# First feed-forward block: up projections as seven half-block products, residual stream in DRAM, down projections between the products

## Chip, cores and metric

The kernel runs on one core of a Trainium2 chip. The metric is device time in microseconds (us), from the program's start to its end. The core has TensorE (PE, matrix products into PSUM), VectorE (DVE), ScalarE (ACT), GpSimd (POOL), and SyncE (SP), whose queue issues the transfers (DMA) between DRAM and the on-chip memory SBUF.

## What is computed

One layer of a diffusion backbone over 512 latent and 256 context tokens of width 1024: a feed-forward half step, a mixing block (gated linear attention and differential attention), a second feed-forward half step and a final norm. The change concerns the first half step alone, which both kinds of token pass with the same weights and with modulations of their own:

```python
def _swiglu(h, w1, w3, w2):
    return (jax.nn.silu(h @ w1) * (h @ w3)) @ w2
...
xl = xl + 0.5 * ml[2] * _swiglu(_modnorm(xl, ffn1_norm[i], ml[0], ml[1]), ffn1_w1[i], ffn1_w3[i], ffn1_w2[i])
xc = xc + 0.5 * mc[2] * _swiglu(_modnorm(xc, ffn1_norm[i], mc[0], mc[1]), ffn1_w1[i], ffn1_w3[i], ffn1_w2[i])
```

`w1` and `w3` are 1024 x 2816, `w2` is 2816 x 1024, all in float32; `ml` and `mc` are the nine adaLN modulations.

## The kernel before

Activations lie with the model dimension on the 128 partitions: `xl` (8 k-tiles x 512 latent tokens) and `xc` (8 x 256 context tokens) stay in SBUF through the block. A float32 product is made of three passes in the float32r format: each operand is split into a high part (ACT copies it) and a low part (DVE subtracts), and PE adds low x high, high x low and high x high. `wload` fetches 512 KB of weights on SP into one of two `raw` buffers, and ACT (L117) and DVE (L118) split them into `whi` and `wlo`, three buffers of each.

The hidden width of 2816 is 22 blocks (f) of 128. For each f, `Ffn.up` runs two weights x 8 k x 3 passes, each a pair of matmuls of 512 and 256 columns (`mm_k`, L246 and L249), into the PSUM tiles `h13`; `act` then forms silu on ACT (L282), the product on DVE (L285) and its parts `gh` and `gl` (L286, L287), which are kept in a ring of eight. The f-blocks are gathered in `CHUNKS` of 6, 6, 5 and 5. Once a chunk is complete, `down` goes over the 8 output tiles m: 5 or 6 f accumulate in a PSUM tile `dn` of two buffers (L123 to L125), and DVE adds it, times the gate, into `xl` and `xc` (L303). The last chunk comes after all up projections, first for the latent tokens, whose norm follows, and then for the context tokens.

Beside this, `more_ada` makes the modulations that are needed later: 56 rows of the adaLN weights come through four buffers `adaw`, and DVE forms 80 dot products from them (`ada_dot`, L133). Ahead of it all the first tokens are normalised and modulated (`mod_h`) k by k, while PE already runs f = 0 on the tiles that are ready. The order of the instructions on each engine is set by a scheduler, which moves weight loads and their splits ahead of other work (`high_priority`); each engine then runs in that order. Tiles with one or two buffers are handed on when their last reader is done.

## Time and profile before

| | us |
|---|---|
| times of three runs | 1791.6, 2190.8 (median), 5782.49 |
| profiled execution, its own time | 1785.35 |
| its span, first to last instruction | 1783.6 |
| PE, DVE, ACT, POOL busy in it | 1738.2, 1000.3, 629.1, 111.6 |

The profile is of one execution, and the durations in this text are from it. The three times differ widely, and the profiled execution's is near the lowest. An engine's busy time is an average over the whole span; what bounds a stage is read from the windows and the waits of that stage. The first feed-forward block takes about the first 605 us: the tokens' norm up to 30, the up projections from there to 555, and the last chunk to 605.

### The profile page before, as it was taken

How to read it: one execution, taken by the hardware profiler on the slowest of the kernel's cores; microseconds unless marked ns; L12 is line 12 of the kernel's file. 1: busy time of each engine (PE TensorE's matmuls, PEld its weight loads, DVE VectorE, ACT ScalarE, POOL GpSimd, SP SyncE). 2: the span in 40 equal slices, each digit the busy share in tenths (PEclk: the TensorE clock that was granted, in tenths of full speed). 3: DMA queues.
4: the chain of work that ended last, by engine and by line, in shares of the span. 5: the costliest groups of instructions: out<-in, count | busy, mean ns of one | idle time of the engine just before them, and what ended most of it. 6: DMA issues, size and time to landing. Idle time of an engine off the chain costs nothing.

```text
span 1783.6 us, 24883 instructions
## 1 busy us (share of the span) xinstructions
PE 1738.2 (97%) x10184; PEld 1523.1 (85%) x10184; DVE 1000.3 (56%) x1666; ACT 629.1 (35%) x940; POOL 111.6 (6%) x190
## 2 busy tenths in 40 slices
PE   6999999999999999999999899999999999999998
PEld 4788888888888889899888789998888988888887
DVE  5554454354445757877755776767655733333445
ACT  3311122111112435555664543434423332222233
POOL 3100000000000400000000212121001100000000
PEclk9999999999999999999999899999999999999999
DMA  8333344244242444423322112122554233333231
GB/s 331 133 117 108 108 139 152 71 135 155 77 154 63 156 133 113 115 82 93 113 83 82 36 60 71 30 67 83 168 159 135 72 92 98 96 94 107 83 115 63
DMA packets 61986, 193.62 MB, mean 109 GB/s; under 512 B 8488, under 2 KB 8744, under 8 KB 60592
## 3 DMA queue, kind: packets, MB, share of 16 engines
q1 hardware_dynamic: 61872, 192.03, 34.2%
q8 instruction: 80, 1.31, 0.3%
q14 instruction: 34, 0.28, 0.0%
HBM read 168.93 MB, written 8.39 MB: 99 GB/s over the span
## 4 chain that ended last, share of the span: by engine, by line
PE 89%; DVE 3%; ACT 1%; issue 1%; POOL 1%; DMA 1%; DVEq 0%; ACTq 0%; POOLq 0%
PE h L249 22%; PE h L246 11%; PE pl L249 8%; PE dn L123 5%; PE dn L124 5%; PE dn L125 5%; PE pl L246 4%; PE pb L249 3%; PE ptm L505 3%; PE ptm L504 3%; PE ptm L506 3%; PE S L613 3%; PE po L249 2%; PE pb L246 1%; PE pa L956 1%; PE pc L249 1%
## 5 line engine op out<-in xcount | busy, mean ns | idle before, releaser
L117 ACT ACTIVATE whi<-raw 128x1024 fp32r<-128x1024 f32 (+2 forms) x246 | 241.1, 983 | 509.1 <-PE dn L125 191.6
L118 DVE TENSOR_TENSOR wlo<-raw,whi 128x1024 fp32r<-128x1024 f32 (+2 forms) x231 | 262.1, 1137 | 219.7 <-ACT whi L117 218.2
L246 PE MATMUL h<-hH,wlo 128*128 128x512 f32 (+1 forms) x704 | 273.3, 388 | 1.9 <-ACT hH L221 1.4
L249 PE MATMUL h<-hL,whi 128*128 128x512 f32 (+1 forms) x704 | 274.5, 390 | 0.6 <-DVE hL L222 0.6
L249 PE MATMUL h<-hH,whi 128*128 128x512 f32 (+1 forms) x704 | 273.2, 388 | 0.0
L249 PE MATMUL h<-hC,whi 128*128 128x256 f32 x704 | 196.9, 280 | 0.0
L123 PE MATMUL dn<-gh,wlo 128*128 128x512 f32 (+1 forms) x568 | 194.5, 343 | 0.6 <-ACT gh L286 0.4
L124 PE MATMUL dn<-gl,whi 128*128 128x512 f32 (+1 forms) x568 | 194.1, 342 | 0.0
L125 PE MATMUL dn<-gh,whi 128*128 128x512 f32 (+1 forms) x568 | 193.6, 341 | 0.0
L246 PEld LDWEIGHTS h<-hH,wlo 128*128 128x128 f32 x704 | 132.2, 188 | 33.1 <-ACT hH L221 2.4
L249 PEld LDWEIGHTS h<-hH,whi 128*128 128x128 f32 x704 | 132.3, 188 | 29.6
L249 PEld LDWEIGHTS h<-hL,whi 128*128 128x128 f32 x704 | 132.3, 188 | 28.2 <-DVE hL L222 1.0
L246 PE MATMUL pl<-hH,wlo 128*128 128x512 f32 x328 | 131.8, 402 | 8.2 <-DVE sg L838 5.1
L285 DVE TENSOR_TENSOR g<-s,h 128x512 f32<-128x512 f32 (+2 forms) x46 | 36.2, 791 | 182.2 <-PE h L249 110.0
L249 PEld LDWEIGHTS h<-hC,whi 128*128 128x128 f32 x704 | 133.0, 189 | 0.7 <-DVE hC L222 0.4
L249 PE MATMUL pl<-hL,whi 128*128 128x512 f32 x328 | 130.6, 398 | 0.0
L249 PE MATMUL pl<-hH,whi 128*128 128x512 f32 x328 | 130.2, 397 | 0.0
L123 PEld LDWEIGHTS dn<-gh,wlo 128*128 128x128 f32 x568 | 107.6, 190 | 13.6 <-ACT gh L286 0.6
L125 PEld LDWEIGHTS dn<-gh,whi 128*128 128x128 f32 x568 | 107.5, 189 | 12.4
L124 PEld LDWEIGHTS dn<-gl,whi 128*128 128x128 f32 x568 | 107.6, 190 | 12.2
L505 PE MATMUL ptm<-wlo,hH 128*128 128x256 f32 x384 | 110.4, 288 | 5.3 <-DVE wlo L118 5.3
L504 PE MATMUL ptm<-whi,hL 128*128 128x256 f32 x384 | 111.7, 291 | 0.0
(267 smaller groups left out, 3315.6 us busy)
## 6 DMA issues: line engine op xcount, KB each, us to landing
raw<-win SPq DMA_DIRECT2D x65, 512.0 KB, 3.6
adaw<-ada SPq DMA_DIRECT2D x56, 512.0 KB, 4.4
raw<-f1w SPq DMA_DIRECT2D x44, 512.0 KB, 3.6
raw<-f2w SPq DMA_DIRECT2D x44, 512.0 KB, 3.5
aw<-ada SPq DMA_DIRECT2D x8, 1024.0 KB, 9.9
raw<-wbr SPq DMA_DIRECT2D x16, 512.0 KB, 3.7
raw<-f1w SPq DMA_DIRECT2D x16, 384.0 KB, 3.4
raw<-wout SPq DMA_DIRECT2D x12, 512.0 KB, 3.5
```

The costliest lines, as they stand in the source:

```text
L117: S.activation(hi[:, :w], raw[:, :w], AF.Copy)
L118: ld = (eng or V).tensor_tensor(lo[:, :w], raw[:, :w], hi[:, :w].bitcast(F32), op=ALU.subtract)
L123: PE.matmul(out_, wl, xh, start=first, stop=False)
L124: PE.matmul(out_, wh, xlo, start=False, stop=False)
L125: PE.matmul(out_, wh, xh, start=False, stop=last)
L246: PE.matmul(dst(o0, n), wl[:, ks], h.at(0, k, o0, n), start=(k == 0), stop=False)
L249: mm = PE.matmul(dst(o0, n), wh[:, ks], h.at(i, k, o0, n), start=False, stop=(k == KT - 1 and i == 0))
L285: self.mark = V.tensor_tensor(g[:, sl], s[:, sl], pts[1][:, sl], op=ALU.mult).ins
L504: PE.matmul(o_, tl, wh[:, cs], start=f, stop=False)
L505: PE.matmul(o_, th, wl[:, cs], start=False, stop=False)
L506: PE.matmul(o_, th, wh[:, cs], start=False, stop=l)
L613: PE.matmul(sp[:, n0:n1], QQ[:, q, c, qs], KK[:, c, n0:n1], start=q == 1, stop=q == 0)
```

## The change

The change makes blocks f = 0 and 1 as before, on two token halves of 384 (256 latent and 128 context tokens each). The other 20 blocks go in ten pairs p. For a pair and one of the two weights (a *unit*; i = 0 is `w1`, i = 1 is `w3`) the operands are cut in 2 x 2: the model dimension in halves of 4 k-tiles, the outputs in two f, the tokens in two halves. The four output quarters come from seven products instead of eight (Strassen's scheme in Winograd's form); a product (`prod`) is 4 k x 3 passes = 12 matmuls of 384 columns. That takes sums and differences of the tokens (`Tq`, formed and split once) and of the weights (`prep`, four DVE additions of 512 columns for each unit, of tiles `X`, `Y`, `L` and `A`, whose splits go to the ring of `whi` and `wlo`, or in `late` to spare room in the tiles that hold the tokens). ACT copies three intermediate states of the accumulation out of PSUM (`c1`, `c2`, `c3`), and DVE adds what is missing to each output.

`xl` and `xc` no longer stay in SBUF. `xs` in DRAM starts as a copy of the input. A down projection now covers a pair (2 f): PE runs it in pieces between the products (0, 4 and 8 pieces in the first three units, 4 in each of the next fifteen, none in the last two), ACT takes each piece times the gate out of PSUM into `yd` (two buffers), and POOL issues a transfer of 384 KB that adds it to `xs` in DRAM. For the last chunk, of four f, `xl` and `xc` are read back from `xs`. `adaw` has two buffers instead of four, the dots' results go to the one-buffer tile `Y` that `prep` uses, and `mod_h` for the first tokens becomes `tok`, with four parts of 384 columns.

The core of the diff:

```diff
+CHUNKS1 = [(f, 2) for f in range(0, 18, 2)] + [(18, 4)]
+TH, LH, CH = T // 2, TL // 2, TC // 2
...
-        w = pool_.tile([P, D], F32, tag="adaw", name=u("adaw"), bufs=4)
+        w = pool_.tile([P, D], F32, tag="adaw", name=u("adaw"), bufs=2)
...
-            jk = pool_.tile([P, D], F32, tag="adaj", name=u("adaj"), bufs=2)
+            jk = junk()
...
+        def tok(k):
+
+            for i, (x_, R_) in enumerate(((xlat[:, k], R[0]), (xctx[:, k], R[1][:, :TC]))):
+                V.scalar_tensor_tensor(x_, x_, modA[:, i, k:k + 1], halves(R_), op0=ALU.mult, op1=ALU.mult)
+                S.activation(x_, x_, AF.Identity, bias=mods[:, k, i:i + 1])
+            for t in range(2):
+                hh, hl = (h1.at(i, k, t * TH, TH) for i in range(2))
+                S.activation(hh, xT[:, k, t], AF.Copy)
+                V.tensor_tensor(hl, xT[:, k, t], hh.bitcast(F32), op=ALU.subtract)
...
+    def sums():
+        return sf.tile([P, D], F32, tag="Y", name=u("Y"), bufs=1)
...
+    def split_q(i):
+        S.activation(Tq[i][0], q_[i], AF.Copy)
+        V.tensor_tensor(Tq[i][1], q_[i], Tq[i][0].bitcast(F32), op=ALU.subtract)
...
+    def prep(p, i):
+        X = wp.tile([P, 1024], F32, tag="raw", name=u("raw"), bufs=RB)
+        L = sf.tile([P, 1024], F32, tag="L", name=u("L"), bufs=1)
+        A = sf.tile([P, 512], F32, tag="A", name=u("A"), bufs=1)
+        Y = sums()
+        l, r = slice(0, 512), slice(512, 1024)
+        with tc.high_priority(offset=WPRI):
+            SY.dma_start(X[:, l], w13[2 * p, i][:, l])
+            SY.dma_start(A, w13[2 * p + 1, i][:, l])
+            SY.dma_start(L[:, r], w13[2 * p + 1, i][:, r])
+            SY.dma_start(L[:, l], w13[2 * p, i][:, r])
+            V.tensor_tensor(X[:, r], A, L[:, r], op=ALU.add)
+            V.tensor_tensor(Y[:, l], X[:, l], X[:, r], op=ALU.add)
+            V.tensor_tensor(Y[:, r], X[:, l], A, op=ALU.add)
+            V.tensor_tensor(A, Y[:, l], L[:, l], op=ALU.add)
+            return ring_w(X), ring_w(Y), L, A
+
+    def late(w):
+        with tc.high_priority(offset=WPRI):
+            return split_w(w[2], spare[1], spare[2]), split_w(w[3], spare[0][:, :512], spare[0][:, 512:])
...
+    def unit(p, i, w, fills, nxt):
...
+        L, S4 = late(w)
+        prod(pa, X, 0, B[0], True)
+        c1 = small("c1")
+        S.activation(c1, pa, AF.Copy)
+        prod(pf, X, 512, Tq[0], True)
+        prod(pa, Y, 0, Tq[3], False)
+        c2 = small("c2")
+        S.activation(c2, pa, AF.Copy)
+        for f in fills[:len(fills) // 2]:
+            f()
+        if not fills:
+            prod(pe, L, 0, B[2], True)
+            out(0, c1, False, pe)
+        prod(pa, Y, 512, Tq[1], False)
+        c3 = small("c3")
+        S.activation(c3, pa, AF.Copy)
+        for f in fills[len(fills) // 2:]:
+            f()
+        nw = prep(*nxt) if nxt else None
+        out(3, c3, True, pf)
+        more_ada()
+        prod(pa, L, 512, Tq[2], False)
+        out(2, None, True, psum=pa)
+        if fills:
+            prod(pe, L, 0, B[2], True)
+            out(0, c1, False, pe)
+        prod(pf, S4, 0, B[3], False)
+        out(1, c2, False, pf)
+        return nw
...
+    def down_add(p, m, wd):
+
+        if m % 4 == 0:
+            wd[0] = wload(w2d[:, 2 * p * D + m * 256:2 * p * D + (m + 4) * 256])
+        y = sr.tile([P, 2, TH], F32, tag="yd", name=u("yd"), bufs=2)
+        for i, seg in enumerate((LAT, CTX)):
+            S.activation(y[:, :, seg[0]], down(2 * p, 2, wd[0], m % 4 * 256, seg), AF.Copy, scale=gate[:, i, m:m + 1])
+        G.dma_start(xs[:, m], y, accum_op=ALU.add)
...
+    with tc.high_priority(offset=WPRI):
+        for m in range(KT):
+            SY.dma_start(halves(xl[:, m, :]), xs[:, m, :, :LH])
+        for m in range(KT):
+            SY.dma_start(halves(xc[:, m, :]), xs[:, m, :, LH:])
```

ACT in the middle of the block, before: the queue holds a silu (`s`), a high part (`gh`) and four weight splits (`whi`) for each f.

```order
L117 ACTIVATE whi418_3000<-raw417_2999 128x1024
L282 ACTIVATE s404_2975<-h13396_2865 128x768
L117 ACTIVATE whi421_3054<-raw420_3053 128x1024
L117 ACTIVATE whi437_3132<-raw436_3131 128x1024
L286 ACTIVATE gh406_2977<-g405_2976 128x768
L282 ACTIVATE s423_3107<-h13415_2997 128x768
L117 ACTIVATE whi440_3186<-raw439_3185 128x1024
L117 ACTIVATE whi456_3264<-raw455_3263 128x1024
L286 ACTIVATE gh425_3109<-g424_3108 128x768
```

ACT in the middle of the block, after; `whi546` and `whi548` are the splits of X and Y, `yd` the evacuations of down pieces:

```order
L491 ACTIVATE whi546_3321<-raw542_3309 128x1024
L570 ACTIVATE c2525_3215<-st522_3171 128x384
L617 ACTIVATE yd529_3223<-dn530_3224,gate_80 128x2x256
L617 ACTIVATE yd529_3223<-dn531_3232,gate_80 128x2x128
L617 ACTIVATE yd532_3241<-dn533_3242,gate_80 128x2x256
L617 ACTIVATE yd532_3241<-dn534_3250,gate_80 128x2x128
L578 ACTIVATE c3535_3271<-st522_3171 128x384
L491 ACTIVATE whi548_3325<-Y545_3312 128x1024
L617 ACTIVATE yd536_3273<-dn537_3274,gate_80 128x2x256
L555 ACTIVATE gh486_2954<-s483_2951 128x384
L617 ACTIVATE yd536_3273<-dn538_3282,gate_80 128x2x128
L617 ACTIVATE yd539_3291<-dn540_3292,gate_80 128x2x256
```

The copies c2 and c3, which PE's next product waits for, now stand behind a weight split, and the evacuations behind the copies, with c3 between the second and the third piece.

DVE in the middle of the block, before: weight splits (`wlo`), the products `g` and `gl`, and dots (`adaj`).

```order
L118 TENSOR_TENSOR wlo265_1841<-raw263_1839,whi264_1840 128x1024
L118 TENSOR_TENSOR wlo268_1895<-raw266_1893,whi267_1894 128x1024
L285 TENSOR_TENSOR g251_1816<-s250_1815,h13243_1706 128x768
L133 SCALAR_TENSOR_TENSOR adaj255_1825,mods_78<-adaw254_1823,sc_89 128x1024
L287 TENSOR_TENSOR gl253_1818<-g251_1816,gh252_1817 128x768
L133 SCALAR_TENSOR_TENSOR adaj256_1827,mods_78<-adaw254_1823,sc_89 128x1024
L133 SCALAR_TENSOR_TENSOR adaj258_1831,mods_78<-adaw257_1829,sc_89 128x1024
L133 SCALAR_TENSOR_TENSOR adaj260_1835,mods_78<-adaw259_1833,sc_89 128x1024
```

DVE at the end of a w3 unit, after; `hC3` and `hH1` receive the late splits of L and A, `raw506` and `Y509` are the sums X and Y for the next unit:

```order
L548 TENSOR_TENSOR c1449_2746<-c1449_2746,pe448_2729 128x384
L492 TENSOR_TENSOR hC3_90<-L468_2867,hL2_89 128x1024
L553 TENSOR_TENSOR s410_2512<-s410_2512,c1449_2746 128x384
L492 TENSOR_TENSOR hH1_88<-A469_2868,hH1_88 128x512
L548 TENSOR_TENSOR c2450_2772<-c2450_2772,st447_2728 128x384
L556 TENSOR_TENSOR gl412_2514<-s410_2512,gh411_2513 128x384
L553 TENSOR_TENSOR s410_2512<-s410_2512,c2450_2772 128x384
L114 TENSOR_TENSOR wlo492_3002<-raw490_3000,whi491_3001 128x1024
L556 TENSOR_TENSOR gl412_2514<-s410_2512,gh411_2513 128x384
L134 TENSOR_TENSOR mods_78<-mods_78,vec_76 128x16 x2
L509 TENSOR_TENSOR raw506_3092<-A508_3094,L507_3093 128x512
L511 TENSOR_TENSOR Y509_3095<-raw506_3092,A508_3094 128x512
```

The late split of A, the outputs c1, c2 and `gl`, the down weights' split and the next unit's first sum now stand in one queue, in this order.

SP at the end of the block, before: the last chunk's weights, then those of the mixing block.

```order
L116 DMA raw_4534<-f1w 128x640
L116 DMA raw_4560<-f1w 128x640
L116 DMA raw_4743<-f1w 128x640
L116 DMA raw_4773<-f1w 128x640
L116 DMA raw_4803<-f1w 128x640
L116 DMA raw_4859<-win 128x1024
L457 DMA xsp<-xl 128x4096
```

SP there, after:

```order
L507 DMA L_4817<-f1w 128x512
L506 DMA A_4818<-f1w 128x512
L508 DMA L_4817<-f1w 128x512
L112 DMA raw_5038<-f1w 128x512
L112 DMA raw_5061<-f1w 128x512
L112 DMA raw_5084<-f1w 128x512
L112 DMA raw_5107<-f1w 128x512
L657 DMA xl<-xs 128x2x256 x8
L659 DMA xc<-xs 128x2x128 x8
L112 DMA raw_5130<-f1w 128x512
L112 DMA raw_5153<-f1w 128x512
```

The 16 reads of `xl` and `xc` stand between the last chunk's weights, ahead of those of its fifth tile and all later ones.

## Rows read from the trace of the kernel before

**Rows 1.** The page, part 1: busy us (share of the span) and instructions of each engine.
```profile
PE 1738.2 (97%) x10184; PEld 1523.1 (85%) x10184; DVE 1000.3 (56%) x1666; ACT 629.1 (35%) x940; POOL 111.6 (6%) x190
```

**Rows 2.** The page, part 4: the chain that ended last, by line.
```profile
PE h L249 22%; PE h L246 11%; PE pl L249 8%; PE dn L123 5%; PE dn L124 5%; PE dn L125 5%; PE pl L246 4%; PE pb L249 3%; PE ptm L505 3%; PE ptm L504 3%; PE ptm L506 3%; PE S L613 3%; PE po L249 2%; PE pb L246 1%; PE pa L956 1%; PE pc L249 1%
```

**Rows 3.** Windows: us, busy time of each engine, granted clock, DMA share, GB/s.
```profile
30.50:58.00 27.50, 25.52 (x190) 18.03 (x187) 18.10 (x36) 13.02 (x23) 8.40 (x20) 1.00 0.52 198
100.00:164.00 64.00, 64.00 (x368) 55.89 (x367) 31.05 (x46) 13.81 (x16) 0.00 (x0) 1.00 0.42 130
30.50:602.00 571.50, 567.62 (x3288) 491.58 (x3285) 284.30 (x423) 130.03 (x168) 22.72 (x30) 1.00 0.38 123
```

**Rows 4.** Waits, 30 to 600 us: total, times, longest.
```profile
ACT s L282 <- PE h L249: 136.2, 22, 7.4
...
PE h L246 <- ACT hH L221: 1.4, 2, 0.8
```

**Rows 5.** Timeline of ACT, 100 to 140 us: start, duration, instruction.
```profile
100.98 0.81 ACT L282 ACTIVATE s<-h 128x768 f32<-128x768 f32 x1 [6.48 <-PE h L249]
...
117.62 0.81 ACT L282 ACTIVATE s<-h 128x768 f32<-128x768 f32 x1 [6.47 <-PE h L249]
```

**Rows 6.** Timeline of PE, 168 to 172 us, a down projection.
```profile
168.02 0.39 PE L123 MATMUL dn<-gh,wlo 128*128 128x512 f32 x1
168.25 0.39 PE L124 MATMUL dn<-gl,whi 128*128 128x512 f32 x1
...
169.50 0.28 PE L124 MATMUL dn<-gl,whi 128*128 128x256 f32 x1
169.62 0.28 PE L125 MATMUL dn<-gh,whi 128*128 128x256 f32 x1
```

**Rows 7.** Groups by line and shape, 0 to 605 us: busy, mean ns, idle before.
```profile
L133 DVE SCALAR_TENSOR_TENSOR adaj<-adaw,sc 128x1024 f32<-128x1024 f32 x80 | 94.4, 1221 | 0.0
...
L118 DVE TENSOR_TENSOR wlo<-raw,whi 128x1024 fp32r<-128x1024 f32 x40 | 50.3, 1258 | 56.3 <-ACT whi L117 56.3
...
L117 ACT ACTIVATE whi<-raw 128x1024 fp32r<-128x1024 f32 x46 | 48.3, 1055 | 131.7 <-PE h L249 80.6 <-PE dn L125 44.4 <-issue 6.6
...
L287 DVE TENSOR_TENSOR gl<-g,gh 128x768 fp32r<-128x768 f32 x21 | 20.1, 955 | 0.2 <-ACT gh L286 0.2
...
L287 DVE TENSOR_TENSOR gl<-g,gh 128x512 fp32r<-128x512 f32 x1 | 0.7, 683 | 0.0
...
L282 ACT ACTIVATE s<-h 128x512 f32<-128x512 f32 x1 | 0.6, 598 | 0.7 <-PE h L249 0.7
...
L287 DVE TENSOR_TENSOR gl<-g,gh 128x256 fp32r<-128x256 f32 x1 | 0.4, 419 | 0.0
...
L282 ACT ACTIVATE s<-h 128x256 f32<-128x256 f32 x1 | 0.4, 380 | 0.0
```

**Rows 8.** DMA issues: KB each, median us from issue to landing.
```profile
adaw<-ada SPq DMA_DIRECT2D x56, 512.0 KB, 4.4
raw<-f1w SPq DMA_DIRECT2D x44, 512.0 KB, 3.6
...
raw<-f1w SPq DMA_DIRECT2D x16, 384.0 KB, 3.4
...
mgd<-mg SPq DMA_DIRECT2D x16, 256.0 KB, 2.0
...
xsp<-xl SPq DMA_DIRECT2D x1, 2048.0 KB, 9.2
...
mgl<-mgd SPq DMA_DIRECT2D x8, 256.0 KB, 3.5
```

**Rows 9.** Timelines of DVE and POOL, 595 to 601 us.
```profile
595.74 0.75 DVE L222 SCALAR_TENSOR_TENSOR hL<-h,mods,hH 128x512 fp32r<-128x512 f32 x1
...
599.26 2.21 DVE L222 SCALAR_TENSOR_TENSOR hL<-h,mods,hH 128x512 fp32r<-128x512 f32 x1
...
598.51 2.41 POOL L118 TENSOR_TENSOR wlo<-raw,whi 128x1024 fp32r<-128x1024 f32 x1 [0.23 <-ACT whi L117]
```

More of the change, by code (lines that the diff above doesn't have):

```diff
@@ L410, in layer, with more_ada @@
-    ffn_es = ExitStack()
-    f1.fp = ffn_es.enter_context(tc.tile_pool(name="ffn1", bufs=1))
-    f1.act(0, pts)
-    lat_part = lambda m: (xl[:, m, :], 0, TL, gate[:, 0, m:m + 1])
-    ctx_part = lambda m: (xc[:, m, :], TL, TC, gate[:, 1, m:m + 1])
-    f1.run(1, lambda m: [lat_part(m), ctx_part(m)], more_ada)
+    def more_ada():
+        if pairs:
+            for j in pairs[:2]:
+                ada_dot(adp, sums, sc, j, (0, 1))
+                if j < 24:
+                    G.tensor_scalar(mods[:, j, :], mods[:, j, :], vec[:, V_BADA + j:V_BADA + j + 1], None,
+                                    op0=ALU.add)
+                    G.tensor_scalar(gate[:, 0:2, j - 16], mods[:, j, :], 0.5, None, op0=ALU.mult)
+            del pairs[:2]
+        else:
+            for j in ones_[:4]:
+                ada_dot(adp, sums, sc, j, (0,))
+            del ones_[:4]
@@ new lines, in late, with prod @@
+    def late(w):
+        with tc.high_priority(offset=WPRI):
+            return split_w(w[2], spare[1], spare[2]), split_w(w[3], spare[0][:, :512], spare[0][:, 512:])
+    def prod(dst, w, c0, op, first):
+        for k in range(4):
+            ks = slice(c0 + k * P, c0 + (k + 1) * P)
+            hi, lo = w[0][:, ks], w[1][:, ks]
+            bh, bl = op[0][:, k, :], op[1][:, k, :]
+            PE.matmul(dst, lo, bh, start=first and k == 0, stop=False, skip_group_check=True)
+            PE.matmul(dst, hi, bl, start=False, stop=False, skip_group_check=True)
+            mm = PE.matmul(dst, hi, bh, start=False, stop=k == 3, skip_group_check=True)
+        return mm.ins
@@ new lines, in layer, with small, out @@
+    ss = {}
+    def small(tag):
+        return sr.tile([P, TH], F32, tag=tag, name=u(tag), bufs=1)
+    def unit(p, i, w, fills, nxt):
+        t = big(u("st"))
+        pa, pf, pe = t[:, :TH], t[:, 512:512 + TH], sm(u("pe"))[:, :TH]
+        X, Y = w[0], w[1]
+        def out(q, c, neg, add=None, psum=None):
+            f, h = 2 * p + q // 2, q % 2
+            sq = s[:, q, :]
+            if i == 0:
+                if psum is None:
+                    V.tensor_tensor(sq, c, add, op=ALU.add)
+                return S.activation(sq, sq if psum is None else psum, AF.Silu, scale=-1.0 if neg else 1.0)
+            if psum is None:
+                V.tensor_tensor(c, c, add, op=ALU.add)
+            src = c if psum is None else psum
+            if neg:
+                V.scalar_tensor_tensor(sq, src, -1.0, sq, op0=ALU.mult, op1=ALU.mult)
+            else:
+                V.tensor_tensor(sq, sq, src, op=ALU.mult)
+            gh, gl = (g[:, h, :] for g in ring[f])
+            S.activation(gh, sq, AF.Copy)
+            V.tensor_tensor(gl, sq, gh.bitcast(F32), op=ALU.subtract)
+        if i == 0:
+            s = ss[p] = thp.tile([P, 4, TH], F32, tag="s", name=u("s"), bufs=2)
+            new_g(2 * p)
+            new_g(2 * p + 1)
+        s = ss[p]
+        L, S4 = late(w)
[27 more added lines that the diff above has]
+        return nw
@@ new lines, in layer, with down_w, down @@
+    w2d = a["f1w2"]
+    def down_w(f0, nf, m, eng=None, hold=None):
+        off = f0 * D + m * nf * P
+        return wload(w2d[:, off:off + nf * P], nf * P, eng, hold)
+    LAT, CTX = (slice(0, LH), TL), (slice(LH, TH), TC)
+    def down(f0, nf, w, c0, seg):
+        (sl, n), (wh, wl) = seg, w
+        pt = gm(u("dn"))
+        o_ = halves(pt[:, :n])
+        for j in range(nf):
+            ks = slice(c0 + j * P, c0 + (j + 1) * P)
+            gh, gl = (g[:, :, sl] for g in ring[f0 + j])
+            mm3(o_, wh[:, ks], wl[:, ks], gh, gl, j == 0, j == nf - 1)
+        return o_
@@ new lines, in down_add @@
+    def down_add(p, m, wd):
[5 more added lines that the diff above has]
+        G.dma_start(xs[:, m], y, accum_op=ALU.add)
+    units = [(p, i) for p in range(1, NF // 2) for i in range(2)]
+    w = prep(*units[0])
@@ L416, in layer @@
+    SY.dma_start(xs, a["x"])
+    wd = [None]
+    downs = [(p, m) for p in range(NF // 2 - 2) for m in range(KT)]
+    for n, un in enumerate(units):
+        if n in (1, 2):
+            more_ada()
+        fills = [lambda d=d: down_add(*d, wd) for d in downs[:(0, 4, 8)[min(n, 2)] if n < 3 else 4]]
+        del downs[:len(fills)]
+        w = unit(*un, w, fills, units[n + 1] if n + 1 < len(units) else None)
+    assert not downs
     assert not pairs and not ones_
@@ L442, in layer @@
     for m in range(KT):
-        f1.down(*CHUNKS[-1], m, [ctx_part(m)], held[m] if m < NH else f1.down_w(*CHUNKS[-1], m, G))
+        w = held[m] if m < NH else down_w(*CHUNKS1[-1], m, G)
+        down_last(w, CTX, xc[:, m, :], gate[:, 1, m:m + 1])
         rc.add(xc[:, m, :], G)
```

136 lines of the change are left out of this document (91 added, 45 removed).

## The prediction

> **What bounds the kernel now.** I read the page's busy times first: TensorE (PE) works 1738.2 us, 97% of the span, VectorE (DVE) 56% [rows 1]. The chain of work that ended last says the same: all its large lines are PE's, and the up projections (h L249 and L246, both half steps together) make 33% of the span [rows 2]. An average over stages proves little, so I cut out the first feed-forward block: the windows show PE busy 567.62 of 571.50 us between 30.5 and 602, and 64.00 of 64.00 in the middle, with DVE at 284 and ACT at 130 of 571 [rows 3]. The waits there agree: what ACT waits for is PE, and the largest sum of PE's own waits is 1.4 us [rows 4]. So in this block every column taken from PE is time, as long as the other engines stay behind it. The granted clock is 1.00 in all these windows, so nothing is to be had from it.
>
> The sum is made against the profiled execution, 1785.35 us. The three times shown lie between 1791.6 and 5782.49; their median of 2190.8 is 23% above the profiled execution, in which I find no idle time to match, so I set 1785.35 in its place (the lowest, 1791.6, is 0.3% above it). Two per cent, about what a measurement of this kernel can tell from no change, is 35.7 us.
>
> **What the change removes.** Twenty of the 22 f-blocks go in ten pairs of two units, one for w1 and one for w3. A unit has 7 products of 12 matmuls of 384 columns, 84 in all; before, the same outputs took 48 pairs of 512 and 256 columns. One f-block takes 16.64 us, from one silu to the next (100.98 to 117.62) [rows 5], that is 0.347 for a pair; and starts lie 0.227 apart for 512 columns, 0.120 for 256 [rows 6], the same sum. 384 columns lie halfway: 0.1735. A unit is then 84 x 0.1735 = 14.57 against 16.64, a gain of 2.07, times 20 = **-41.4**. With 384 at the rate of 256 it would be 0.180 and -30, at the rate of 512 0.170 and -47. Blocks 0 and 1 keep their columns (384+384 for 512+256), and so do the down projections.
>
> So the gain is at most 2.6%, and the rest is a question of what the other engines lose again. For their work: a DVE pass of 256, 512, 768 and 1024 columns takes 0.419, 0.683, 0.955 and 1.258, an ada dot 1.221; ACT from PSUM 0.380 and 0.598 for 256 and 512, a split of 1024 1.055 [rows 7]. Hence estimates of 0.55 for 384 columns on DVE, 0.49 on ACT, 1.76 for 1536 on DVE.
>
> **The load per unit.** PE, with four pieces of down projection of 6 x 0.227 + 6 x 0.120 = 2.08: 14.57 + 8.33 = 22.9. DVE (w3 unit): four weight sums 2.73, three splits 3.77, S4's split 0.68, the down weights' split 1.26, eleven output passes 6.05, four dots 4.88: 19.4; a w1 unit about 15. ACT: splits 1.06 x 4 + 0.6, three copies and four outputs 3.4, eight evacuations 3.9: about 12. All lie under 22.9, so none is the new bound by its sum. What counts is the order.
>
> **The chain inside a unit.** The buffers L and A are single, and hH's spare half takes S4's split. So when the last product of a unit ends: ACT hH 0.6, DVE hH 0.68, then SP may load A for the unit after, X's sum 0.68, X's split 1.06 on ACT, and behind that on the same queue c2 (0.49) and the evacuations yd. PE needs the second dn buffer back some 8.3 us after the unit's start (three products 6.25 and a first piece 2.08). Without the load and five hand-overs (an estimate of 0.1 each) the chain is 4.0 long, so the load may take 4.3. No 256 KB weight load is in the trace; the nearest rows are 512 KB at 3.6, 384 KB at 3.4, and 256 KB in another pattern at 3.5 [rows 8]. That fits with 0.7 to 0.9 to spare when nothing is in the way. But DVE runs in order, and X's sum stands before the outputs while dots of 1.2 stand ahead: I take 0.4 per unit for the first eight of the sixteen units from the third to the eighteenth, with two ada transfers each. In the other eight four ada rows of 512 KB (4.4 each [rows 8]) share the queue with L and A, and the load is then 1 to 2 us longer, past what there is to spare: 0.9 per unit. So **+10.4**, with ends 0 (the cover holds) and 24 (1.5 for each of 16).
>
> **The accumulating write.** 72 times GpSimd (POOL) issues a 384 KB write that adds to DRAM, where DVE used to add into SBUF (L303). y has two buffers, so a write must be done when ACT wants its buffer again: about 5.2 us later in the tight places (two pieces of 2.08 and the products between). If it is late, ACT stops with c3, the splits and the outputs behind it, dn stays full, and PE stops. No POOL transfer and no adding one is in the trace, so it is bounded from both sides: a plain 256 KB write to DRAM lands in 2.0, a 384 KB load in 3.4, one of 2 MB in 9.2 [rows 8]. I take 3.4 to 5 (a read on top of a write of this size), so it is covered: **0**. Every us beyond 5.5 costs about 1 in each of 17 units.
>
> Evacuation itself moves from DVE to ACT: 0.60 against a cover of 0.72 for the 256-wide half; that is near, and I let it hold (0); each 0.1 that it lacks costs 0.1 in each of 72 pieces, 7 in all.
>
> **Start, seam and end.** The first tokens: two ACT copies of 384 more in the first k, +1.0; the sums of x for the seven products (1.76 each) stand on DVE ahead of the last tokens, +1: **+2** (0 to 4). Between f=1 and the first two units there are no down pieces to hide the copies and splits, and DVE has four splits of 1.76 and the weight sums to clear: Y's split late by 1.1, c2 and c3 uncovered 0.8, X of the next unit late by 1.7: **+3.6** (1 to 7). The last two units have no pieces either: L's split 1.3, X 1.7, c3 0.75: **+3.75** (1.5 to 6). The end: x comes back from DRAM in 16 pieces, 3 MB; the first piece waits for the buffers of the last unit and lands some 6 us after it, so the third down piece of the last chunk stalls 1.4 on its dn buffer; and the later weight loads stand behind the 16 on SP, ready at about 18 where PE is at 15: 2.9. **+4.3** (2 to 8). The 3.1 MB copy of x into xs is queued behind the first unit's weights, at a DMA share of about a half [rows 3]; I cost it at nothing, since its readers come a unit later; else 1 to 2 more at the seam.
>
> Sum: 1785.35 - 41.4 + 10.4 + 0 + 2 + 3.6 + 3.75 + 4.3 = 1768.0. I forecast **1768 us**: a small gain, within what can be told.
>
> **The rivals.**
> - All cover holds. The steady units cost nothing and start, seam and end stand at their low ends (0 + 1 + 1.5 + 2): 1785.35 - 41.4 + 4.5 = 1748, a gain of 2.1%. For it: DVE and ACT have 4 to 10 us free in every unit. Against: the order of the queues, as above.
> - The load of A and L, or DVE's order, costs 1.5 us in every unit: 1768 + 24 - 10.4 = 1782, next to nothing gained. For it: single buffers, adaw cut from four to two, and dots whose result now goes to the tile Y that prep needs too. Against: no engine's sum passes PE.
> - Slower: the accumulating write. If one takes as long as the row of 2 MB, 9.2, that is 3.7 over the cover of 5.5 in 17 units: 1768 + 63 = 1831. It eats the forecast's gain (17) from 6.5 us on, and passes 2% at 8.6. For it: it must read before it writes, and it goes through POOL, while DVE and POOL slow each other in the rows: a DVE pass of 0.75 takes 2.21 when POOL runs a split of 2.41 beside it [rows 9]. Against: 256 KB in 2.0.
> - POOL is kept from its part by DVE. In rows 9 the stretched DVE pass ends 0.55 after POOL's, as if it had waited for it (599.26 + 2.21 against 598.51 + 2.41); if each write's issue waits likewise for one or two DVE passes, it is 1.4 to 2.8 longer than 3.4 to 5, so up to 2.3 over the cover: 17 units at about 2, 1768 + 34 = 1802.
>
> The last one is a rule of the Trainium skill too, "SBUF — State Buffer", SBUF: two separate sides: POOL writes the descriptors of its transfers over a port pair that it shares with DVE, and a DVE pass in a two-port mode locks it out; it gives 620 ns alone against 3100 overlapped. Rows 9 agree in kind (DVE's pass slowed, not POOL's transfer), and no run here shows a transfer. By that rule 2.5 us come on top of the 5, 2 over the cover, and the time is the same 1802. The page "DMA: Bandwidth & Descriptors", Anatomy of one DMA — SWDGE (gpsimd) path, gives 2.0 us plus bytes over 436 GB/s, which for 384 KB is an estimate of 2.9 us for a plain POOL transfer, and by it the sum would stay as it is.
>
> **How the numbers follow.** Forecast (1755 to 1779) 0.48; all cover holds 0.17; load chain 0.14; POOL held back 0.09; slow accumulating write 0.12. The likeliest gives 1768. The range takes in 1745 (all cover holds and the gain a little over) and 1817: below lies 0.05, above 0.12. Faster than 1749.6: most of the cover case, 0.14. Slower than 1821: most of the slow write, a little of the held POOL and of the chain, 0.12. Within: 0.74.
>
> **What would show it.** In the profile after: products 0.1735 apart, and a unit near 23.5 us where it would be 22.9 without waits; the PE waits, small and on ACT (c2, X's split) or DVE's hH, more in the late units; POOL's writes landing in 3.4 to 5. It is wrong if ACT's yd waits on a DMA, if PE waits on yd in each unit, or if DVE's pass lengths grow beside POOL. A unit under 23.0 throughout would mean that I saw waits where there are none.

## The result, and the profile after

The change makes the kernel slower: 1852.2 us (1849.35 to 1854.84) against 1788.95 and 1791.6 of before, ratio 1.0346, 95% interval 1.0310 to 1.0381. The forecast was 1768, and the range ended at 1817. Four executions of before that stand beside this take 1788.95 to 5782.49; the two far above 1800 are disturbed and left out.

The profiled execution has a span of 1847.6 us, 64.0 over the 1783.6 of before. First the page: the busy times [rows 1], the granted clock in its 40 slices, and the chain by line [rows 2]; behind it the clock row of before.

```profile
PE 1736.8 (94%) x9944; PEld 1547.4 (84%) x9944; DVE 1104.5 (60%) x1834; ACT 781.2 (42%) x1236; POOL 185.2 (10%) x278
...
PEclk9998999999998999999999989999999999999999
...
PE h L248 8%; PE pl L248 8%; PE h L245 4%; PE pl L245 4%; PE ptm L737 3%; PE pb L248 3%; PE ptm L736 3%; PE ptm L738 3%; PE dn L119 3%; PE dn L120 3%; PE dn L121 3%; PE S L845 2%; PE po L248 2%; PE pb L245 1%; PE pa L1188 1%; PE pc L248 1%
```

```profile
PEclk9999999999999999999999899999999999999999
```

PE is as busy as before (1736.8 against 1738.2), in a longer span: 94%. The clock row has an 8 in the second half both times, behind this block; the two in the first third (slices at 139 to 185 and 554 to 600 us) are new. The chain has lost the products of the pairs from its first places; they are spread over many lines now. The window on the middle of the block shows it better; columns as in [rows 3]:

```profile
100.00:550.00 450.00, 413.99 (x2205) 381.02 (x2204) 276.49 (x416) 202.57 (x334) 68.97 (x84) 0.96 0.75 177
```

PE, which hardly ever stood here before, idles 36 of 450 us, at a mean clock of 0.96, and the DMA engines are busy 0.75 of the time where they were 0.38 over the block. Now what PE waits for between 30 and 640 us (total, times, longest), against 1.4 for the largest before [rows 4]:

```profile
PE pe L524 <- DVE hC L492: 15.0, 4, 4.0
PE dn L119 <- ACT yd L617: 14.8, 9, 3.4
PE st L524 <- ACT c L570: 10.1, 5, 4.4
PE h L245 <- ACT hL L400: 4.6, 2, 3.2
```

Four markers split the 64.0 us. The first product starts at 84.9, the place of the second block's end before is 76.0: **+8.9** (start). The last chunk's first matmul comes at 615.2 against 555.3; the down work of one more f (8 x 3 x 0.347 = 8.3) is in the pairs now, so the pairs and their pieces cost 530.3 - 479.3 - 8.3 = **+42.7** where a gain was forecast. From there to the mixing block's first product: 48.2 against 46.7 - 8.3 = 38.4, **+9.8**. The rest is **+2.6**. Inside the pairs, ACT's copies c1 mark each unit (timeline of ACT; start, duration):

```profile
350.11 0.49 ACT L566 ACTIVATE c<-st 128x384 f32<-128x384 f32 x1 [0.81 <-PE st L526]
...
373.77 0.47 ACT L566 ACTIVATE c<-st 128x384 f32<-128x384 f32 x1
...
408.43 0.47 ACT L566 ACTIVATE c<-st 128x384 f32<-128x384 f32 x1
...
431.53 0.47 ACT L566 ACTIVATE c<-st 128x384 f32<-128x384 f32 x1
```

From 350.11 to 373.77 is a w1 unit of 23.7; the w3 unit behind it takes 34.7, the next w1 unit 23.1. All four late w3 units take 34.4 to 35.2, the second unit of all 35.4 and the third, with eight pieces, 42.1. The others with four pieces take 23.1 to 25.8. So the loss sits in six units and in what surrounds the pairs, not evenly in all.

What makes a late w3 unit long shows in two places. At its end, where the next unit begins (timeline of DVE, then of PE; the idle time before and what ended it in brackets):

```profile
399.27 1.23 DVE L129 SCALAR_TENSOR_TENSOR Y<-adaw,sc 128x1024 f32<-128x1024 f32 x1 [1.78 <-DMA adaw<-ada]
...
403.60 1.23 DVE L129 SCALAR_TENSOR_TENSOR Y<-adaw,sc 128x1024 f32<-128x1024 f32 x1 [2.62 <-DMA adaw<-ada]
...
404.75 1.22 DVE L492 TENSOR_TENSOR hC<-L,hL 128x1024 fp32r<-128x1024 f32 x1
...
402.18 0.34 PE L526 MATMUL st<-hH,whi 128*128 128x384 f32 x1
406.02 0.69 PE L524 MATMUL pe<-hL,hC 128*128 128x384 f32 x1 [3.51 <-DVE hC L492]
```

Two dots wait on DVE for their adaw row, 1.78 and 2.62 us; behind them in DVE's queue stands the late split of L (hC, 404.75). The next unit's product on L is second in PE's order, and PE stands from 402.5 to 406.0. At the same unit's front (DVE; SP; ACT; PE):

```profile
373.44 1.23 DVE L129 SCALAR_TENSOR_TENSOR Y<-adaw,sc 128x1024 f32<-128x1024 f32 x1 [0.66 <-DMA adaw<-ada]
...
375.73 0.69 DVE L492 TENSOR_TENSOR hH<-A,hH 128x512 fp32r<-128x512 f32 x1
...
376.45 0.33 SPq L506 DMA_DIRECT2D A<-f1w  x1
...
381.99 1.06 ACT L491 ACTIVATE whi<-raw 128x1024 fp32r<-128x1024 f32 x1 [4.54 <-DVE raw L509]
382.95 0.47 ACT L570 ACTIVATE c<-st 128x384 f32<-128x384 f32 x1
...
379.93 0.28 PE L121 MATMUL dn<-gh,whi 128*128 128x256 f32 x1
383.47 0.44 PE L524 MATMUL st<-T,wlo 128*128 128x384 f32 x1 [3.26 <-ACT c L570]
```

The load of A is issued only at 376.45, since it waits for A's late split (hH, 375.73), which had stood behind two dots as well; X's sum and split follow, ACT's c2 stands behind the split, and PE waits for it from 380.2 to 383.5. In the second and third late w3 unit c2 is ahead of X's split and the first copy yd stands behind it; there PE waits for yd, 3.0 and 3.4 us. The gap at a unit's front is the chain of the forecast, priced at 0.9 per unit; the one at its end, PE's wait for the late split of L, has no term there in these units. The late w3 units are about 11 over the 23.5 of a unit without waits (below).

Part of these 11 is no wait. Windows around the gap that ends at 406.0 (columns as in [rows 3]; the clock stands before the DMA share):

```profile
398.00:402.00 4.00, 4.00 (x25) 4.00 (x24) 1.71 (x3) 1.74 (x3) 0.00 (x0) 1.00 0.97 257
402.00:404.00 2.00, 0.51 (x3) 0.19 (x2) 0.41 (x1) 0.00 (x0) 0.00 (x0) 1.00 1.03 373
404.00:406.00 2.00, 0.00 (x0) 0.00 (x0) 2.00 (x4) 0.00 (x0) 0.00 (x0) 0.88 0.71 207
406.00:408.00 2.00, 1.98 (x6) 1.98 (x7) 2.00 (x5) 0.00 (x0) 0.00 (x0) 0.50 0.73 245
408.00:410.00 2.00, 2.00 (x10) 2.00 (x10) 1.18 (x3) 1.31 (x3) 0.00 (x0) 0.77 0.93 212
410.00:412.00 2.00, 2.00 (x13) 2.00 (x12) 1.62 (x4) 0.53 (x2) 0.00 (x0) 1.00 0.51 193
```

PE idles from 402.5 to 406.0, and the clock granted behind that is 0.50, 1.2 GHz in place of 2.4, and back at 1.00 some 3 us after PE has started again. Between 100 and 640 us PE has twelve gaps of 2.0 to 4.4 us, and the clock twelve stretches at 0.50, one beside each gap. Summed over windows of 2 us from 60 to 640, (1 - clock) x PE's busy time is 24 us, an estimate, and 0 before; PE's idle time in the same windows is 58.4 against 3.7.

### The profile page after: what moved, and what is told of

Same layout as the page of the kernel before. It is cut to its first block, busy times and chain, and to the rows that moved or that the text cites. A ratio compares the mean times of both kernels' runs of the same rounds, so it can differ in the third digit from the quotient of the medians.

```text
span 1847.6 us, 25207 instructions
## 1 busy us (share of the span) xinstructions
PE 1736.8 (94%) x9944; PEld 1547.4 (84%) x9944; DVE 1104.5 (60%) x1834; ACT 781.2 (42%) x1236; POOL 185.2 (10%) x278
## 3 DMA queue, kind: packets, MB, share of 16 engines
q0 software_dynamic: 10368, 28.32, 10.3%
## 4 chain that ended last, share of the span: by engine, by line
PE 61%; DVE 3%; DMA 2%; ACT 1%; issue 1%; POOL 1%; DVEq 0%; ACTq 0%; POOLq 0%; SPq 0%
PE h L248 8%; PE pl L248 8%; PE h L245 4%; PE pl L245 4%; PE ptm L737 3%; PE pb L248 3%; PE ptm L736 3%; PE ptm L738 3%; PE dn L119 3%; PE dn L120 3%; PE dn L121 3%; PE S L845 2%; PE po L248 2%; PE pb L245 1%; PE pa L1188 1%; PE pc L248 1%
## 5 line engine op out<-in xcount | busy, mean ns | idle before, releaser
L114 DVE TENSOR_TENSOR wlo<-raw,whi 128x1024 fp32r<-128x1024 f32 (+3 forms) x185 | 210.6, 1141 | 169.0 <-ACT whi L113 167.7
L113 ACT ACTIVATE whi<-raw 128x1024 fp32r<-128x1024 f32 (+3 forms) x200 | 197.2, 990 | 263.8 <-PE dn L121 70.5
L248 PE MATMUL h<-hL,whi 128*128 128x512 f32 (+2 forms) x384 | 145.1, 378 | 2.0 <-DVE hL L401 2.0
L248 PE MATMUL h<-hH,whi 128*128 128x512 f32 (+2 forms) x384 | 144.4, 376 | 0.0
L245 PE MATMUL h<-hH,wlo 128*128 128x512 f32 (+2 forms) x368 | 139.3, 379 | 1.9 <-ACT hH L400 0.9
L129 DVE SCALAR_TENSOR_TENSOR Y<-adaw,sc 128x1024 f32<-128x1024 f32 x80 | 97.8, 1222 | 30.3 <-DMA adaw<-ada 29.0
L617 ACT ACTIVATE yd<-dn,gate 128x512 f32<-128x512 f32 (+1 forms) x144 | 79.5, 578 | 81.0 <-PE dn L121 32.3
L738 PE MATMUL ptm<-whi,hH 128*128 128x256 f32 x384 | 110.8, 289 | 0.0
L618 POOL DMA_DIRECT2D xs<-yd x72 | 62.4, 867 | 377.0 <-ACT yd L617 377.0
L524 PE MATMUL st<-T,wlo 128*128 128x384 f32 x240 | 85.1, 354 | 10.5 <-ACT c L570 10.1
```

Of the source, the lines that this page charges most:

```text
L113: S.activation(hi[:, :w], raw[:, :w], AF.Copy)
L114: ld = (eng or V).tensor_tensor(lo[:, :w], raw[:, :w], hi[:, :w].bitcast(F32), op=ALU.subtract)
L129: V.scalar_tensor_tensor(jk, w, 1.0, sc[:, i, :], op0=ALU.mult, op1=ALU.mult, accum_out=mods[:, j, i:i + 1])
L245: PE.matmul(dst(o0, n), wl[:, ks], h.at(0, k, o0, n), start=(k == 0), stop=False)
L248: mm = PE.matmul(dst(o0, n), wh[:, ks], h.at(i, k, o0, n), start=False, stop=(k == KT - 1 and i == 0))
L524: PE.matmul(dst, lo, bh, start=first and k == 0, stop=False, skip_group_check=True)
```

## The experiments

Theory A: the adaw rows, bunched on two buffers, put dots that wait for transfers ahead of the late splits on DVE, and so hold PE. Theory B: the adding writes do it, by their own latency or by what they take from the DMA engines. Theory C: the granted clock falls because PE idles, and that adds to each wait. The table gives each kernel's median time, its ratio to the kernel before with the 95% interval, and the mean time of a unit in us in the profiled execution, taken from c1 to c1: the second, the third, the fourth to the eleventh, and of the late ones w1 and w3. The times lie within 10 us of each other per kernel, but for fills_even (1827 to 1847). The profiled execution lies 5 to 6 us above the median in rows_planned and as much below it in planned_even and spread_xc_later, in the others within 3.

| kernel | us | ratio | 2nd | 3rd | 4th-11th | late w1 | late w3 |
|---|---|---|---|---|---|---|---|
| changed | 1852.2 | 1.0346 (1.0310-1.0381) | 35.4 | 42.1 | 24.4 | 23.1 | 34.8 |
| late_dots_out | 1807.4 | 1.0112 (1.0089-1.0135) | 35.5 | 41.8 | 24.3 | 23.6 | 24.0 |
| plain_write | 1816.8 | 1.0168 (1.0145-1.0192) | 33.3 | 35.1 | 23.7 | 22.5 | 30.9 |
| filler | 1853.5 | 1.0366 (1.0342-1.0389) | 35.2 | 41.5 | 24.4 | 27.3 | 33.1 |
| rows_apart | 1838.6 | 1.0274 (1.0245-1.0303) | 38.8 | 40.4 | 26.8 | 25.0 | 25.8 |
| adaw3 | 1830.4 | 1.0243 (1.0225-1.0261) | 32.2 | 44.6 | 24.6 | 22.5 | 30.4 |
| fills_even | 1829.6 | 1.0267 (1.0210-1.0324) | 17.3 | 29.8 | 25.1 | 22.2 | 32.7 |
| rows_planned | 1823.8 | 1.0209 (1.0181-1.0236) | 32.5 | 42.6 | 26.2 | 24.3 | 24.6 |
| planned_even | 1816.7 | 1.0161 (1.0138-1.0184) | 14.6 | 31.0 | 25.3 | 26.0 | 24.5 |
| planned_spread | 1797.1 | 1.0061 (1.0043-1.0080) | 14.6 | 28.6 | 24.7 | 23.6 | 25.0 |
| spread_plain | 1778.1 | 0.9953 (0.9937-0.9968) | 14.6 | 28.6 | 23.6 | 23.5 | 23.8 |
| spread_xc_later | 1792.7 | 1.0039 (1.0026-1.0052) | 14.6 | 28.6 | 24.7 | 23.6 | 24.6 |
| spread_sums_late | 1796.4 | 1.0056 (1.0041-1.0071) | 14.6 | 28.6 | 25.0 | 23.8 | 24.8 |

From fills_even on, but not in rows_planned, the second unit has no pieces and the third four in place of eight.

**late_dots_out** leaves out the 32 late dots and their loads; those modulations are set to zero, so it computes less.

```diff
-            for j in ones_[:4]:
-                ada_dot(adp, sums, sc, j, (0,))
             del ones_[:4]
```

> Leaves out the 32 dots of the eight late calls and their loads (those modulations are set to zero). Theory A (four adaw rows through two buffers put dots that wait for a transfer ahead of the late split of L and of A on DVE): the four w3 units that take 35 us fall to 23 to 25, the waits on hC vanish there, span 1847.6 - 42 to - 48 = about 1800 to 1806. Theory B (the accumulating writes hold yd and fill the DMA engines): adaw is only a part of the traffic, those units stay above 31, span above 1830.

The late w3 units fall to 24.0 and the time by 45, as theory A has it. PE's waits between 80 and 615 us:

```profile
PE dn L119 <- ACT yd L616: 9.9, 9, 3.8
...
PE st L523 <- ACT c L569: 1.5, 3, 0.6
```

None on hC is left, and c2 costs 1.5 where it cost 10.1. Dots and loads go together here, so this run alone doesn't part the dots' work, their wait for rows and what the rows take from other loads.

**plain_write** lets the writes overwrite, so the sum in `xs` is lost.

```diff
-        G.dma_start(xs[:, m], y, accum_op=ALU.add)
+        G.dma_start(xs[:, m], y)
```

> The 72 writes to xs overwrite instead of adding (the residual sum is lost). Theory B: the writes land in about 3 instead of 5.4, the DMA share between 100 and 550 us falls from 0.75 towards 0.5, and the span falls by 50 or more. Theory A: the waits on yd shrink in the third unit (8 pieces), 5 to 8 us, and the loads of adaw, L and A become shorter by about 1, which takes 2 to 3 from each of the four long units: span down by 12 to 25.

The fall of 35 lies between the two theories' figures. The window of the middle, then the issue rows of this kernel and of the changed one (times issued, KB, median us to landing):

```profile
100.00:550.00 450.00, 427.14 (x2331) 392.45 (x2332) 293.13 (x443) 216.37 (x353) 49.17 (x88) 0.98 0.55 187
```

```profile
adaw<-ada SPq DMA_DIRECT2D x56, 512.0 KB, 4.6
xs<-yd POOLq DMA_DIRECT2D x72, 384.0 KB, 2.9
...
A<-f1w SPq DMA_DIRECT2D x20, 256.0 KB, 3.4
```

```profile
adaw<-ada SPq DMA_DIRECT2D x56, 512.0 KB, 5.6
xs<-yd POOLq DMA_DIRECT2D x72, 384.0 KB, 5.4
...
A<-f1w SPq DMA_DIRECT2D x20, 256.0 KB, 4.3
```

A write that adds lands in 5.4 us, one that overwrites in 2.9, and the DMA share goes from 0.75 to 0.55 (the packets of POOL's queue take 10.3% and 4.0% of 16 engines' span, for the same 28.32 MB). The third unit gains 7, the late w3 units 4. Both causes are real, and they meet: the adding writes slow the adaw rows (5.6 against 4.6; 4.4 before) for which the dots wait, and the loads of A (4.3 against 3.4).

**filler** adds 18 matmuls, whose result is overwritten, in three late w1 units.

```diff
+        if i == 0 and p in (7, 8, 9):
+            for q in range(18):
+                PE.matmul(pe, X[0][:, :P], B[0][0][:, 0, :], start=q == 0, stop=q == 17, skip_group_check=True)
```

> Adds 18 matmuls of 384 columns whose result is overwritten, in three late w1 units, 14 of them (2.4 us) where PE idles 3.5 to 4.0 us for hC. Theory C (the long idle time itself is what lowers the granted clock afterwards, and about 2 us are lost to that at each): the granted clock behind the three gaps stays at 1.00 in more of the slices, each of these pairs of units is shorter by 1 to 2 us although PE does 3.1 us more work in it, span down by 3 to 6. If the clock falls for another reason (the transfers, the other engines): span the same or up by 1 to 3 (the four matmuls that lie elsewhere), clock as before.

No gain: 1.3 us up in the median, inside the scatter of the changed kernel's times. The wait only changed its name: in these units PE now waits for c1, three times, 13.4 us in all. But PE does 54 matmuls more (54 x 0.175 = 9.4), and the estimate of what the lower clock costs falls from 24 to 19, which is the direction of theory C. The experiment doesn't settle C by its time.

**rows_apart** spreads the rows, three per unit in two places, from the first unit to the last.

```diff
-            for j in pairs[:2]:
+            for j in pairs[:1]:
...
-        more_ada()
+        rows(2)
...
         out(2, None, True, psum=pa)
+        rows(1)
```

> All rows of adaw and all 80 dots stay, but one to three rows per unit from the first to the last, in two places, in place of none to four in one place. Theory A: the long units fall from 35 to 24 to 27, and the span by 30 to 45. If the number of dots or the one-buffer tile Y is what holds the splits up, and not the bunching of the rows on two buffers: the loss is only spread over more units, span down by less than 12.

The late w3 units come down to 25.8, but three units of the first half, where up to six dots stand in place of four, go to 28.6, 30.5 and 33.1, and the time falls by 14 only, between the figures of the two statements. Three rows of two dots are too many for one unit; this holds for the second statement in part.

**adaw3** has three buffers for two.

```diff
-        w = pool_.tile([P, D], F32, tag="adaw", name=u("adaw"), bufs=2)
+        w = pool_.tile([P, D], F32, tag="adaw", name=u("adaw"), bufs=3)
```

> Only change: three adaw buffers for two. Theory A, in the form that the second pair of the four rows has to wait for a buffer and then for its transfer: three of four rows are there early, one still waits, so the four long w3 units fall from 35 to 27 to 30 and the span by 20 to 32. If it is the number of dots ahead of the late splits on DVE that costs, and not their wait for a transfer: the long units stay above 32 and the span falls by less than 12.

As theory A has it: -22, late w3 units 30.4, a little over the 27 to 30; no wait on hC is left. What is left are c2 and the pieces' yd (PE's waits, 60 to 615 us):

```profile
PE st L524 <- ACT c L570: 15.6, 8, 3.9
PE dn L119 <- ACT yd L617: 14.7, 10, 6.6
```

A, whose load X's split and so c2 wait for, lands only after 4.4 to 6.1 us in the late units here. That is the forecast's reason (the rows share the queue), at a higher price; a third buffer doesn't remove it.

**fills_even** places four pieces in each unit from the third to the last.

```diff
-        if n in (1, 2):
+        if n == 3:
             more_ada()
-        fills = [lambda d=d: down_add(*d, wd) for d in downs[:(0, 4, 8)[min(n, 2)] if n < 3 else 4]]
+        fills = [lambda d=d: down_add(*d, wd) for d in downs[:4 if n > 1 else 0]]
```

> Down pieces 4 in each unit from the third to the last in place of 4, 8, then 4; the extra calls for dots in the second and third unit become one in the fourth. The second and third units took 35.4 and 42.1 where 23.6 and 32 would do without waits. If the eight adding writes in a row (their 5.4 us against two yd buffers) and the eight dots of the second unit are what costs: the two units and the two last ones together become 14 to 20 shorter, span down by 12 to 18. If it is the seam itself (the sums of x and the first splits, which stay): span down by less than 6.

The second and third unit lose 30 us, of which 8 pieces (16.7) come back in the last two units: 14 net; the time falls by 23, in runs that scatter more than the others'. The dots of the first units move with the pieces here. From rows_planned to planned_even only the pieces move, and the two units lose 29.5, 13 net: the pieces' bunching was a cause of its own.

**rows_planned** loads at most three rows per unit one unit ahead into three buffers, and holds the dots behind the late splits.

```diff
         L, S4 = late(w)
+        with tc.issue_after(lastv[0]):
+            ada_dots()
+        ada_load()
...
-        more_ada()
```

> Three adaw buffers, at most three rows per unit, loaded one unit ahead, and their dots put behind the late splits of L and A on DVE; same 80 dots, pieces as in the changed kernel. Theory A: no unit of the late eight is over 25, no wait on hC is left, span down by 40 to 48, as if the late dots were not there (1806). Theory that DVE's work as such is too much: the late units are 26 or more, span down by 30 or less.

The late units behave as forecast (24.6, no wait on hC), but the time falls by 28 and not by 40 to 48: in nearly every unit there is now a wait on yd, so the first half is 1.8 longer per unit (PE's waits, 80 to 640 us):

```profile
PE dn L119 <- ACT yd L630: 31.0, 18, 5.7
```

**planned_even** is rows_planned with fills_even's table. 

> rows_planned and the even pieces together. If the two losses are separate, the gains add: 40 to 48 and 12 to 18, span about 1783 to 1795, level with the kernel before. If they share a cause (DVE's queue in the first units), the sum is under 45 and the span over 1802.

It misses: 1816.7. The losses are not separate, but what they share is not DVE's queue. PE's waits (60 to 615 us),

```profile
PE dn L119 <- ACT yd L630: 24.1, 17, 2.5
```

and what ACT's copies wait for:

```profile
ACT yd L630 <- DMA xs<-yd: 33.7, 21, 3.3
```

Once the units are shorter, the third piece of a unit comes back to a yd buffer whose adding write is still under way.

**planned_spread** sets the four pieces of a unit behind four products, one by one.

```diff
-        for f in fills[:len(fills) // 2]:
+        for f in fills[:1]:
...
-        for f in fills[len(fills) // 2:]:
+        for f in fills[1:2]:
...
+        for f in fills[2:3]:
+            f()
         if fills:
             prod(pe, L, 0, B[2], True)
             out(0, c1, False, pe)
+        for f in fills[3:]:
+            f()
```

> planned_even, and the four down pieces of a unit stand one by one behind four products in place of two and two. In planned_even nearly every unit has one wait of 1.4 to 2.5 us on yd, whose buffer an adding write of 5.3 us still holds. If that is the spacing against two yd buffers: the waits on yd fall under 6 us in all, units go from 25.2 to 23.6 to 24, span from 1809 to 1780 to 1790. If ACT's order is what is late and not the write: units stay at 25, span as planned_even or more.

The waits on yd are gone (0.2 us), the time falls by 20, and the span of 1792.8 ends just over the forecast's 1780 to 1790. The window of the middle:

```profile
100.00:550.00 450.00, 434.04 (x2422) 403.77 (x2421) 302.43 (x456) 219.80 (x364) 71.94 (x82) 1.00 0.79 185
```

The clock is 1.00 again, the DMA share 0.79. What is left is c2, 11.2 us in nine places of 1.1 to 1.6.

**spread_plain** is planned_spread with plain_write's edit. 

> planned_spread with writes that overwrite in place of adding (the residual sum is lost): what the adding is still worth once its latency is covered. If only its latency counted: the same as planned_spread within 5 us. If the transfers that it holds up on the DMA engines count as well: 8 to 20 us less than planned_spread.

```profile
100.00:550.00 450.00, 445.09 (x2493) 416.21 (x2494) 311.87 (x474) 227.29 (x379) 52.22 (x86) 1.00 0.56 190
```

19 us less: so the adding writes cost beyond their own latency. In the profiled executions 14.6 of it lie before the mixing block (606.6 against 592.0). What X's sum waits for, and with it c2, planned_spread and then spread_plain, 80 to 640 us:

```profile
DVE raw L520 <- DMA A<-f1w: 26.2, 16, 2.4
PE st L535 <- ACT c L584: 11.2, 9, 1.6
```

```profile
DVE raw L520 <- DMA A<-f1w: 8.9, 10, 1.5
PE st L535 <- ACT c L584: 1.9, 4, 0.6
```

So most of it goes by way of the loads: A's and L's median landing falls from 2.9 and 3.5 to 2.7 and 3.1. PE is busy 445 of 450 us here, and a unit still takes 23.6: that is about what the work itself costs.

**spread_xc_later** moves the reads of xc behind the last chunk's latent pieces.

```diff
     with tc.high_priority(offset=WPRI):
         for m in range(KT):
             SY.dma_start(halves(xl[:, m, :]), xs[:, m, :, :LH])
-        for m in range(KT):
-            SY.dma_start(halves(xc[:, m, :]), xs[:, m, :, LH:])
...
+    for m in range(KT):
+        SY.dma_start(halves(xc[:, m, :]), xs[:, m, :, LH:])
     R2 = big(u("R"))
```

> planned_spread, and the eight reads of xc stand behind the last chunk's latent pieces and not ahead of its later weights. The end's wait of 2.6 to 3.1 us on the split of those weights was put down to this queue: the last chunk is 2 to 4 shorter, span down by as much from planned_spread. If xc then comes late for the context pieces: 0 or worse.

Inconclusive: 4 us less in the median, but the wait that it was to remove was already gone in planned_spread, and the trace shows 1 us less up to the mixing block; the rest lies behind it, where nothing was changed. It is the fastest of the variants that compute the whole, and still 0.4% slower than before, a difference well under the 2%.

**spread_sums_late** also holds the sums of x behind the last token's split (a mark, the split's instruction, that they are issued after). 

> spread_xc_later, and the sums of x for the products are held behind the last token's split on DVE. In the changed kernel the first product starts 8.7 us later than the same place of before, of which 8.6 are PE waits on hL and hH of the last tokens. If the sums ahead of them are the reason: 3 to 6 of these vanish, and the first units lose less than 2 of it again, span down by 2 to 5. If tok's own four parts are: no change, or the first units wait for the sums and it is slower by 1 to 3.

The first c1 comes at 84.2 against 86.9, and the first unit takes 19.1 against 17.1: moved, not saved. The sums are a third of the start's loss at most. In the changed kernel 2.1 of the 8.9 are there already at the first up product (32.6 us against 30.5), and behind PE's wait of 3.2 for hL the clock is 0.50 from 64.2 to 67.6. tok's four parts or the chain through them may be the rest, which no run separates.

## Why the prediction was wrong

**The bound** was right: PE's time is the block's time, and the other engines cost only where PE waits for them.

**The gain of 41.4** was too large a term. A unit was priced at 22.9 without waits; where PE hardly waits (spread_plain) it is 23.6, 0.1 of it a wait, against 24.97 of before (16.64 + 8.33): 23.5, so 20 units give 29. Timeline of PE in the changed kernel:

```profile
204.00 0.34 PE L524 MATMUL st<-T,wlo 128*128 128x384 f32 x1
204.18 0.34 PE L525 MATMUL st<-T,whi 128*128 128x384 f32 x1
...
209.16 0.28 PE L121 MATMUL dn<-gh,whi 128*128 128x256 f32 x1
209.30 0.44 PE L524 MATMUL st<-T,wlo 128*128 128x384 f32 x1
209.88 0.50 PE L119 MATMUL dn<-gh,wlo 128*128 128x512 f32 x1
210.21 0.39 PE L120 MATMUL dn<-gl,whi 128*128 128x512 f32 x1
```

In a run of like matmuls 384 columns mostly take 0.173 to 0.177, in the mean 0.175 and not 0.1735: 0.13 per unit. And changes cost: from 209.16 to 210.21 pass 1.05 us for 256, 384 and 512 columns that take 0.52 in a run (0.120 + 0.1755 + 0.2275); PE is idle in 0.14 of the rest. In spread_plain, between 130 and 530, the intervals at changes between the products' tiles and dn exceed their columns by 5.4 us in 17 units, 0.3 per unit with the waits; another 0.2 lies scattered. The step that failed is the one that took starts in a run of like matmuls for the price of an order that changes tiles about eleven times a unit (193 in these 17).

**The chain inside a unit (+10.4)** is the main failure. The mechanism was the right one for the front of a unit (late split of A, load of A and L, X's split, c2), the size was not, and PE's wait for the late split of L had no term: 10.4 in sixteen units was forecast, the excess of these over 23.5 (31.8 for the third, which has eight pieces) is 62, the lower clock included. "0.9 per unit" for the late ones had the load 1 to 2 us longer because adaw shares the queue; A's landing, 4.3 in the median over the block, is just what the cover allowed. The forecast knew that DVE runs in order, but took the dots ahead at their own length of 1.2. The step that failed is that it gave them no wait: a dot that waits for its row makes everything behind it wait, the splits of L and of A first, and the product on L stands early in PE's order. adaw3 shows that the waits on hC, 15.0, come from the rows; those on c2 stay there, since A lands late, and go in rows_planned (0.6), which also shows that the dots as such fit.

**The accumulating write (0)** was forecast at 3.4 to 5 and measured 5.4 in the median, up to 9.1, where it was to begin to cost at 5.5. One of the forecast's signs of being wrong is there (ACT's waits, 80 to 640 us):

```profile
ACT yd L617 <- DMA xs<-yd: 29.8, 13, 5.9
```

Where pieces are two and two, overwriting saves 0.8 per unit (fourth to eleventh, plain_write). Eight pieces in the third unit were not in the estimate (7 us, plain_write), nor what an adding write takes from the other loads (most of the 19 us between planned_spread and spread_plain). The rival that ended slower named one of two causes, at another price: it needed 8.6, and the kernel passed 2% at 5.4, since the rows cost as well; without the late dots (1.0112) or with plain writes (1.0168) it lies below 2%.

**The rival that POOL is kept from its part by DVE** didn't happen. POOL's part of a write takes 0.85 to 1.06 us in all 72 (0.54 to 0.78 in plain_write), with DVE busy beside it or not; the rival had 1.4 to 2.8 on top. A dot takes 1.222 (page of the changed kernel) against 1.221 before [rows 7], with POOL's writes beside it, and a plain write lands in 2.9:

```profile
L129 DVE SCALAR_TENSOR_TENSOR Y<-adaw,sc 128x1024 f32<-128x1024 f32 x80 | 97.8, 1222 | 30.3 <-DMA adaw<-ada 29.0
```

The lock that the Trainium skill tells of ("SBUF — State Buffer", SBUF: two separate sides) shows in no write of this block. The Trainium skill ("SBUF — State Buffer", Who interferes with whom) says that tensor_tensor has no two-port mode and, with both inputs in SBUF, contends with GpSimd's reads alone; that agrees with the sums, splits and outputs here, beside which POOL's part is no longer, and the forecast had passed it over. For a plain transfer of this size the Trainium skill ("DMA: Bandwidth & Descriptors", Anatomy of one DMA — SWDGE (gpsimd) path) gives an estimate of 2.9 us, and plain_write agrees with 2.9; a write that adds, at 5.4, is another matter.

**Start, seam and end.** The start was forecast at +2 and is 8.9 (spread_sums_late). The end was forecast at +4.3 and is 9.8: its two waits came about as forecast (1.6 on xl, 2.9 on the later weights, 1.4 and 2.9 in the sum); left out were 1.4 and 2.7 on xc (1.1 before) and about 1.7 of lower clock behind the second wait (0.50 from 634.2 to 637.6). The last two units, +3.75, are about right (waits of 1.5, 1.2 and 0.7). The second unit, in the seam, had eight dots and four pieces on top of the seam's own splits: 11.9 over 23.5, where 3.6 was the whole seam.

**Left out altogether**: the clock. "Nothing is to be had from it" was read from a block without waits; it can be lost. What it took is an estimate from the windows, and no experiment isolates it. In sum for the pairs, 84.9 to 615.2: 41.4 - 29 = 12 for the products, 21 of the 24 us of clock, and 50 us of PE's gaps (530.3 less the sum of PE's busy time) where 17.8 were forecast, 32: together 65, and the pairs are 66.4 off the forecast (42.7 against -23.7).

The fastest variant that computes the whole comes to 1.0039, 5 us behind before by the medians. planned_spread with writes that don't add is 0.5% faster than before, so adding in DRAM eats what was left of the seven products' gain.
